# Four steps instead of one for the decays of the first attention group in a hybrid decoder layer

## The chip, the cores and the metric

The kernel runs on one core of a Trainium2 chip. The metric is the device time of one execution in microseconds (us), as the median of several runs. A profile is one execution recorded by the hardware; its span goes from the first to the last instruction of the core. TensorE (PE in the profile) multiplies matrices and writes to PSUM, which has eight tiles here; VectorE (DVE) and ScalarE (ACT) do elementwise work; SyncE (SP) issues most loads. Each engine works through its own queue in order, and they wait for each other through semaphores.

## The reference

One layer of a decoder, for 256 positions of width 2048, in float32: a SwiGLU half-step, a token mixer, a second SwiGLU half-step, each with norms ahead and behind. The mixer projects its input by one wide matrix and runs two causal mixers, GLA (4 heads, key width 128) and HGRN2 (8 heads). The lines that matter here are the decays of GLA:

```
proj = u @ w_in
(g_q, g_k, g_v, g_out, g_code, h_q, h_f, ...) = jnp.split(proj, offsets, axis=-1)
gla_log_a = jax.nn.log_sigmoid(g_code @ gla_w_gk_up + gla_b_gk) / GLA_GATE_NORMALIZER   # 16
o_gla = chunked_gated_linear_attention(split_heads(g_q * (GLA_DK ** -0.5), GLA_HEADS), ...)
```

The kernel works with the decays exp(gla_log_a) themselves, transposed, so that the key dimension lies on the partitions.

## The kernel before, in words

All large products are made in three matmuls of 512 columns: the float32 weights are split into a high part (whi, a copy on ScalarE, L151) and a rest (wlo, a subtraction on VectorE, L153), and so is the activation; `mm3` (L155 to L159) adds high by high (L157), low by high (L158) and high by low (L159).

In the mixer, `gemm_pair` (L329) makes two blocks of 512 output columns in one pass, for both halves of the positions, in four PSUM tiles c00, c10, c01, c11. It runs over the inner dimension in units of 256. A plain step of a unit takes one weight block of 1024 columns (a split on ScalarE, a split on VectorE) and twelve matmuls. Some units, `seven` (L265), use fewer products in the manner of Strassen: 21 matmuls from sums of weight blocks. Such a unit makes `whi` by L278 and L282, the sums `wsum` on VectorE (L243), their high parts `wsumh` on ScalarE (L280 for two thirds, L284 for the last), and then the rests on VectorE, `wlo` twice and `wsuml`. The first `seven` of a pass also takes four more PSUM tiles, p1, p6, p5 and p7 (L291 to L293), and with c they are all eight. So whatever side work holds in these four tiles has to be read out before the first products on p can start. The weights land in a ring of five raw tiles (`raw`, loaded by SP: L133 for a plain block, L272 to L275 for the four blocks of a `seven`), and a raw tile is free for the next load when its split on VectorE is done.

Side work is written as Python generators. `Side.spawn` (L61) runs a generator to its first `yield`; each `side.pump()` (L65), which stands behind the steps of the matmul loops, lets every light generator run on to its next `yield`. So the yields say between which matmul steps a piece of side work is emitted. The framework then orders the instructions of each engine, so the built order of an engine is near to the order of emission but not the same.

Around the change three such generators are light at the same time, during the pass `two(O_GK, O_GV, ...)` (L1167):

- `gla_decays` (L1023): it transposes the 16 code columns (L1035), multiplies them with `gk` (L1043) into two PSUM tiles y, and makes the decays: e = |y| (L1048, ScalarE), m = min(y, 0)/16 (L1050, VectorE), e = exp(-e) (L1053), e = ln(1 + e) (L1055), m = m - e/16 (L1057, VectorE), and fT = exp(m) in four pieces (L1062). A load of ScalarE's function table stands ahead of Ln and another ahead of the second Exp.
- `transposed` (L833), twice, for the queries of the second mixer: four transposes into a PSUM tile (L397) and a copy to hqT on ScalarE (L839).
- `lc_row` (L1082): two matmuls with a matrix of ones (L1093, L1094) into a PSUM tile, and a copy `lcr` (L1096).

Once fT is there, VectorE multiplies the queries of the first mixer with it (qT, L890).

Of the kernel before, what the change touches and what calls it, by code (L numbers as in the profile page):

```python
# [86 lines left out]
def kernel(ctx: ExitStack, tc: tile.TileContext, a: dict, out: bass.AP):  # L87
# [19 lines left out]
    def ps_tile(s="ps"):  # L107
        return psum.tile([P, CB], F32, tag="ps", name=nm(s))
# [292 lines left out]
    def tiles4(x):  # L401
        return x.rearrange("p (k c) -> p k c", c=P)
# [383 lines left out]
    def mixer(x, rs, ready, following):  # L786
        xl = lhs_of(x)
        w_in = a["w_in"]
        with ExitStack() as mctx:
# [5 lines left out]
            def blk(s, dt=F32):  # L795
                return b2.tile([P, CB], dt, tag="b", name=nm(s), bufs=33)
# [33 lines left out]
            def mark(*tiles):  # L830
                laid.update(id(x) for x in tiles)
# [191 lines left out]
            def gla_decays(code, fT):  # L1023


                cs = blk("code")
                for t in range(NT):
                    nc.scalar.activation(cs[:, t * 16:(t + 1) * 16], code[t][:, :16], AF.Copy,
                                         scale=rs[t])
                ct = blk("codeT")  # L1030
                nc.vector.memset(ct[0:17, :NT * P], 1.0)
                yield
                tp = ps_tile()
                for t in range(NT):
                    nc.tensor.transpose(tp[:16, t * P:(t + 1) * P], cs[:, t * 16:(t + 1) * 16], ident)  # L1035
                nc.vector.tensor_copy(ct[0:16, :NT * P], tp[:16, :NT * P])
                yield
                ys = []
                for g in range(2):
                    y = ps_tile()  # L1040
                    for j in range(2):
                        i = 2 * g + j
                        nc.tensor.matmul(y[:, j * 256:(j + 1) * 256], lhsT=gk[:, i * P:(i + 1) * P],  # L1043
                                         rhs=ct[0:17, :NT * P], start=True, stop=True)
                    ys.append(y)
                es, ms = [blk("e") for _ in range(2)], [blk("m") for _ in range(2)]
                for y, e in zip(ys, es):
                    nc.scalar.activation(e, y, AF.Abs)  # L1048
                for y, m in zip(ys, ms):
                    nc.vector.tensor_scalar(m, y, 0.0, 1.0 / GATE_NORMALIZER,  # L1050
                                            op0=ALU.min, op1=ALU.mult)
                for e in es:
                    nc.scalar.activation(e, e, AF.Exp, scale=-1.0)  # L1053
                for e in es:
                    nc.scalar.activation(e, e, AF.Ln, bias=1.0)  # L1055
                for e, m in zip(es, ms):
                    nc.vector.scalar_tensor_tensor(m, e, -1.0 / GATE_NORMALIZER, m,  # L1057
                                                   op0=ALU.mult, op1=ALU.add)
                for g, m in enumerate(ms):
                    mv = m.rearrange("p (h t c) -> p h t c", t=NT, c=P)  # L1060
                    for t in range(NT):
                        nc.scalar.activation(tiles4(fT[t])[:, 2 * g:2 * g + 2, :], mv[:, :, t, :],  # L1062
                                             AF.Exp)
                mark(*fT)
# [51 lines left out]
            side.spawn(operand_sums(x, new_part, sums, False))  # L1116
            hq0 = gemm_block(w_in, O_CODE, 16 + CB, xl)
            side.spawn(gla_decays([hq0[t][0] for t in range(NT)], fT))
            half = (16 + CB) // 2
            for t in range(NT):  # L1120
# [239 lines left out]
```

## Time and profile before

| | |
|---|---|
| runs before, us | 2083.17, 2084.87, 2084.71 |
| median, us | 2084.71 |
| span of the profiled execution, us | 2083.3 |
| instructions | 29324 |
| TensorE busy, us (share of the span) | 2069.5 (99%) |
| VectorE busy, us | 1855.3 (89%) |
| ScalarE busy, us | 1240.8 (60%) |
| mean granted clock of TensorE | 0.998 |
| HBM read and written, MB | 406.11, 4.19 |

The page gives the span of the profiled execution and no other time for it; the median of the runs lies 1.4 us above it. Busy time of TensorE counts matmuls whose ends overlap the next start, so the distance of their starts says more than their durations. In a row of a timeline stand the start in us from the span's start, the duration, the engine, the line, the operation with output and inputs by the names of the program, and in brackets the idle time of the engine ahead of it and what ended it. Waits are listed as who waited for whom, the sum, the count and the longest.

### The profile page before, as it was taken

What the parts mean: (1) busy time and instruction counts of PE and PEld (TensorE: products, weight loads), DVE (VectorE), ACT (ScalarE), POOL (GpSimd) and SP (SyncE); (2) the same over time, 40 slices, a digit from 0 to 9 for tenths busy, and PEclk for the clock granted to TensorE, in tenths of its full rate; (3) what the DMA queues carried; (4) which work ended last, traced back from release to release, by engine and by line L of the source; (5) the groups of instructions that cost most, each with busy time, mean ns of one, the idle gap of its engine ahead of it and who ended that gap; (6) DMA issues with size and microseconds to landing.
All of it is one profiled execution on the core that took longest, in us unless ns stands there. A gap on an engine that the chain in (4) does not pass through costs nothing.

```text
span 2083.3 us, 29324 instructions
## 1 busy us (share of the span) xinstructions
PE 2069.5 (99%) x10509; PEld 1722.0 (83%) x10509; DVE 1855.3 (89%) x2187; ACT 1240.8 (60%) x1670; POOL 40.7 (2%) x87
## 2 busy tenths in 40 slices
PE   9999999999999999999999999999999999999998
PEld 7888888898888888878888888888888888898886
DVE  7898999989899779989999897578999989999896
ACT  6555656566666575576655554465555655666663
POOL 1000000000000100000000000010000000000000
PEclk9999999999999999999999999999999999999999
DMA  8666656667767466555566566755665656576663
GB/s 267 184 209 201 213 187 197 210 185 223 216 191 235 148 201 210 159 172 188 178 195 195 178 220 216 221 182 171 222 197 188 207 187 225 164 238 202 202 206 128
DMA packets 200666, 412.24 MB, mean 198 GB/s; under 512 B 18036, under 2 KB 26423, under 8 KB 200520
## 3 DMA queue, kind: packets, MB, share of 16 engines
q1 hardware_dynamic: 194896, 401.80, 60.9%
q10 hardware_dynamic: 5624, 8.57, 1.4%
q8 instruction: 82, 1.34, 0.3%
q14 instruction: 64, 0.52, 0.1%
HBM read 406.11 MB, written 4.19 MB: 197 GB/s over the span
## 4 chain that ended last, share of the span: by engine, by line
PE 96%; ACT 2%; DVE 1%; issue 1%; DMA 0%; POOL 0%; SPq 0%; DVEq 0%; POOLq 0%; ACTq 0%
PE c L157 22%; PE c L159 21%; PE c L158 21%; PE p L159 5%; PE p L157 5%; PE p L158 5%; PE mm L157 3%; PE mm L159 3%; PE mm L158 3%; PE ps L397 2%; PE acc L157 1%; PE acc L158 1%; PE acc L159 1%; PE ps L905 0%; DVE h L510 0%
## 5 line engine op out<-in xcount | busy, mean ns | idle before, releaser
L151 ACT ACTIVATE whi<-raw 128x1024 fp32r<-128x1024 f32 (+3 forms) x498 | 511.0, 1033 | 284.8 <-PE c L158 116.8
L153 DVE TENSOR_TENSOR wlo<-raw,whi 128x1024 fp32r<-128x1024 f32 (+3 forms) x498 | 587.7, 1190 | 85.5 <-ACT whi L151 84.2
L157 PE MATMUL c<-whi,xhi 128*128 128x512 f32 (+1 forms) x1270 | 495.8, 391 | 0.1
L159 PE MATMUL c<-wlo,xhi 128*128 128x512 f32 (+1 forms) x1270 | 490.9, 387 | 0.0
L158 PE MATMUL c<-whi,xlo 128*128 128x512 f32 (+1 forms) x1270 | 490.6, 386 | 0.0
L243 DVE TENSOR_TENSOR wlo<-raw,whi 128x1024 fp32r<-128x1024 f32 (+1 forms) x252 | 294.5, 1202 | 12.2 <-ACT whi L278 6.1
L159 PEld LDWEIGHTS c<-wlo,xhi 128*128 128x128 f32 x1270 | 238.5, 188 | 47.5 <-DVE wlo L153 0.3
L157 PEld LDWEIGHTS c<-whi,xhi 128*128 128x128 f32 x1270 | 238.6, 188 | 46.3 <-ACT xhi L469 0.5
L158 PEld LDWEIGHTS c<-whi,xlo 128*128 128x128 f32 x1270 | 238.7, 188 | 45.0
L282 ACT ACTIVATE whi<-raw 128x1024 fp32r<-128x1024 f32 (+1 forms) x126 | 131.8, 1046 | 203.9 <-DVE raw L243 80.9
L243 DVE TENSOR_TENSOR wsuml<-wsum,wsumh 128x1536 fp32r<-128x1536 f32 (+1 forms) x126 | 218.1, 1731 | 36.8 <-ACT wsumh L284 36.5
L157 PE MATMUL c<-whi,hkhi 128*128 128x512 f32 x558 | 217.0, 389 | 0.0
L159 PE MATMUL c<-wlo,hkhi 128*128 128x512 f32 x558 | 216.8, 388 | 0.0
L158 PE MATMUL c<-whi,hklo 128*128 128x512 f32 x558 | 216.7, 388 | 0.0
L280 ACT ACTIVATE wsumh<-wsum 128x1024 fp32r<-128x1024 f32 (+1 forms) x126 | 131.6, 1045 | 107.4 <-DVE wsum L243 70.5
L278 ACT ACTIVATE whi<-raw 128x1024 fp32r<-128x1024 f32 (+1 forms) x126 | 131.6, 1044 | 103.0 <-PE c L158 87.7
L243 DVE TENSOR_TENSOR wsum<-raw,raw 128x1024 f32<-128x1024 f32 (+1 forms) x126 | 151.8, 1205 | 21.6 <-DMA raw<-in_ffn_w_down_dram 18.1
L159 PEld LDWEIGHTS c<-wlo,hkhi 128*128 128x128 f32 x558 | 104.7, 188 | 21.6
L158 PEld LDWEIGHTS c<-whi,hklo 128*128 128x128 f32 x558 | 104.7, 188 | 21.4
L157 PEld LDWEIGHTS c<-whi,hkhi 128*128 128x128 f32 x558 | 104.7, 188 | 21.1
L243 DVE TENSOR_TENSOR c<-c,psum 128x512 f32<-128x512 f32 (+1 forms) x135 | 86.5, 683 | 11.8 <-PE c L159 11.4
L243 DVE TENSOR_TENSOR wsum<-raw 128x512 f32<-128x512 f32 (+1 forms) x126 | 86.0, 683 | 3.5
(347 smaller groups left out, 3119.4 us busy)
## 6 DMA issues: line engine op xcount, KB each, us to landing
raw<-in_ffn_w_down_dram SPq DMA_DIRECT2D x124, 512.0 KB, 4.5
raw<-in_w_in_dram SPq DMA_DIRECT2D x104, 512.0 KB, 4.5
raw<-in_ffn_w_up_dram SPq DMA_DIRECT2D x97, 512.0 KB, 4.6
raw<-in_ffn_w_gate_dram SPq DMA_DIRECT2D x96, 512.0 KB, 4.7
raw<-in_ffn_w_gate_dram SPq DMA_DIRECT2D x128, 256.0 KB, 3.7
raw<-in_w_in_dram SPq DMA_DIRECT2D x128, 256.0 KB, 3.5
raw<-in_ffn_w_up_dram SPq DMA_DIRECT2D x126, 256.0 KB, 3.8
raw<-in_ffn_w_down_dram SPq DMA_DIRECT2D x96, 256.0 KB, 4.2
```

What stands on the lines that cost most here:

```text
L151: last[0] = nc.scalar.activation(hi, src, AF.Copy)
L153: nc.vector.tensor_tensor(lo, src, hi.bitcast(F32), op=ALU.subtract)
L157: nc.tensor.matmul(ps, lhsT=xhi, rhs=whi, start=start, stop=False)
L158: nc.tensor.matmul(ps, lhsT=xlo, rhs=whi, start=False, stop=False)
L159: nc.tensor.matmul(ps, lhsT=xhi, rhs=wlo, start=False, stop=stop)
L243: return nc.vector.tensor_tensor(o, x, y, op=op)
L278: nc.scalar.activation(ahi, ra, AF.Copy)
L280: nc.scalar.activation(hi[:, 0:2, :], wsum[:, 0:2, :], AF.Copy)
L282: nc.scalar.activation(bhi, rb, AF.Copy)
L397: end = nc.tensor.transpose(dst_ps[:, i * P:(i + 1) * P], src[:, i * P:(i + 1) * P], ident)
```

## The change

Three yields are put into `gla_decays`. What was emitted as one piece behind the second pump is now emitted in four: the two products, |y| and m; then the first Exp; then Ln; then m and the last Exp. The generators of the queries and of `lc_row`, which come behind it in the list, run their own next pieces in between.

```
@@ -1049,10 +1049,13 @@
                 for y, m in zip(ys, ms):
                     nc.vector.tensor_scalar(m, y, 0.0, 1.0 / GATE_NORMALIZER,
                                             op0=ALU.min, op1=ALU.mult)
+                yield
                 for e in es:
                     nc.scalar.activation(e, e, AF.Exp, scale=-1.0)
+                yield
                 for e in es:
                     nc.scalar.activation(e, e, AF.Ln, bias=1.0)
+                yield
                 for e, m in zip(es, ms):
                     nc.vector.scalar_tensor_tensor(m, e, -1.0 / GATE_NORMALIZER, m,
                                                    op0=ALU.mult, op1=ALU.add)
```

Behind these lines all line numbers are up to 3 higher in the changed kernel (L1057 for Ln, L1060 for m, L1065 for the last Exp, L1099 for lcr). The number behind a name tells tiles of the same name apart, and it can differ between the two builds for the same tile. No instruction is added or taken away on any engine, and SP's order is the same.

ScalarE, in the pass of `two(O_GK, O_GV, ...)`, before, from the first Exp of the decays to the split of the next `seven`; e and fT are the decays, whi_7044 and whi_7046 the high parts of that `seven`:

```order
L1053 ACTIVATE e_6881<-e_6881 128x512
L1055 ACT_TABLE_LOAD
L1055 ACTIVATE e_6880<-e_6880 128x512
L1055 ACTIVATE e_6881<-e_6881 128x512
L278 ACTIVATE whi_7044<-raw_7035 128x1024
L1062 ACT_TABLE_LOAD
L1062 ACTIVATE fT_6439<-m_6882 128x256
L1062 ACTIVATE fT_6440<-m_6882 128x256
L1062 ACTIVATE fT_6439<-m_6883 128x256
L1062 ACTIVATE fT_6440<-m_6883 128x256
L839 COPY hqT_6780<-ps_6898 128x512
L839 COPY hqT_6781<-ps_6904 128x512
```

The same place on ScalarE now:

```order
L1054 ACTIVATE e_6881<-e_6881 128x512
L839 COPY hqT_6780<-ps_6888 128x512
L839 COPY hqT_6781<-ps_6894 128x512
L1099 COPY lcr_6903<-ps_6900 128x512
L1057 ACT_TABLE_LOAD
L1057 ACTIVATE e_6880<-e_6880 128x512
L1057 ACTIVATE e_6881<-e_6881 128x512
L278 ACTIVATE whi_7044<-raw_7035 128x1024
L1065 ACT_TABLE_LOAD
L1065 ACTIVATE fT_6439<-m_6882 128x256
L1065 ACTIVATE fT_6440<-m_6882 128x256
L1065 ACTIVATE fT_6439<-m_6883 128x256
```

The three copies stood behind the last Exp (lcr follows the second copy before as well) and now stand between the first Exp and Ln's table load. Both builds have two table loads here. Behind the Exp group the order is now wsumh_7038 (L280), whi_7046 (L282), wsumh_7038 (L284), whi_7081; before it was whi_7046, whi_7081 and then the two of wsumh_7038.

TensorE, in the same pass, before: the rows from the last product on c ahead of the first products on p6, p5 and p7 (p_1487, p_1488, p_1489) of the pass's first `seven`:

```order
L159 MATMUL c_1452_6832<-wlo_7002,xhi_1326_6187 128x512
L157 MATMUL c_1452_6832<-whi_7001,xhi_1326_6187 128x512
L157 MATMUL p_1487_6975<-whi_6962,xs_6539 128x512
L158 MATMUL p_1487_6975<-whi_6962,xs_6540 128x512
L159 MATMUL p_1487_6975<-wlo_6963,xs_6539 128x512
L157 MATMUL p_1488_6976<-wsumh_6954,xs_6539 128x512
L158 MATMUL p_1488_6976<-wsumh_6954,xs_6540 128x512
L159 MATMUL p_1488_6976<-wsuml_6955,xs_6539 128x512
L157 MATMUL p_1489_6977<-wsumh_6954,xs_6539 128x512
L158 MATMUL p_1489_6977<-wsumh_6954,xs_6540 128x512
L159 MATMUL p_1489_6977<-wsuml_6955,xs_6539 128x512
L158 MATMUL c_1452_6832<-whi_7001,xlo_1327_6188 128x512
```

TensorE now, from the last product on p1 (p_1486) on:

```order
L159 MATMUL p_1486_6968<-wlo_6955,xhi_1311_6092 128x512
L157 MATMUL p_1487_6969<-whi_6956,xs_6539 128x512
L158 MATMUL p_1487_6969<-whi_6956,xs_6540 128x512
L159 MATMUL p_1487_6969<-wlo_6957,xs_6539 128x512
L157 MATMUL p_1488_6970<-wsumh_6948,xs_6539 128x512
L158 MATMUL p_1488_6970<-wsumh_6948,xs_6540 128x512
L159 MATMUL p_1488_6970<-wsuml_6949,xs_6539 128x512
L157 MATMUL p_1489_6971<-wsumh_6948,xs_6539 128x512
L158 MATMUL p_1489_6971<-wsumh_6948,xs_6540 128x512
L159 MATMUL p_1489_6971<-wsuml_6949,xs_6539 128x512
L159 MATMUL c_1452_6832<-wsuml_6949,xhi_1326_6187 128x512
L157 MATMUL c_1450_6830<-whi_7001,xhi_1311_6092 128x512
```

The nine products on p6, p5 and p7 have moved forward by eleven matmuls: they stood among the twelve of the plain step on whi_7001 and now stand right behind the products on p1, ahead of that step. After them come, in both builds, the rest of the twelve on whi_7001, the twelve on whi_7019, and the products of the next `seven`, whose p1 on whi_7044 comes first.

VectorE, before, at the splits of that next `seven`:

```order
L890 TENSOR_TENSOR qT_6437<-qT_6437,fT_6439 128x512
L890 TENSOR_TENSOR qT_6438<-qT_6438,fT_6440 128x512
L243 TENSOR_TENSOR wlo_7047<-raw_7036,whi_7046 128x1024
L153 TENSOR_TENSOR wlo_7082<-raw_7079,whi_7081 128x1024
L243 TENSOR_TENSOR wsuml_7039<-wsum_7037,wsumh_7038 128x1536
L153 TENSOR_TENSOR wlo_7100<-raw_7097,whi_7099 128x1024
L243 TENSOR_TENSOR wsum_7117<-raw_7115,raw_7116 128x1024
```

VectorE now:

```order
L890 TENSOR_TENSOR qT_6437<-qT_6437,fT_6439 128x512
L890 TENSOR_TENSOR qT_6438<-qT_6438,fT_6440 128x512
L243 TENSOR_TENSOR wlo_7047<-raw_7036,whi_7046 128x1024
L243 TENSOR_TENSOR wsuml_7039<-wsum_7037,wsumh_7038 128x1536
L153 TENSOR_TENSOR wlo_7082<-raw_7079,whi_7081 128x1024
L153 TENSOR_TENSOR wlo_7100<-raw_7097,whi_7099 128x1024
L243 TENSOR_TENSOR wsum_7117<-raw_7115,raw_7116 128x1024
```

wsuml_7039 has moved ahead of wlo_7082. Ahead of these rows a third of wsum_7037 is now made ahead of the decays' m instead of behind it. From the end of this pass on, the order of all engines is the same in both builds.

More of the change, by code (lines that the diff above doesn't have):

```diff
@@ L1051, in gla_decays @@
                                             op0=ALU.min, op1=ALU.mult)
+                yield
                 for e in es:
                     nc.scalar.activation(e, e, AF.Exp, scale=-1.0)
+                yield
                 for e in es:
                     nc.scalar.activation(e, e, AF.Ln, bias=1.0)
+                yield
                 for e, m in zip(es, ms):
```

## The prediction

> **What bounds the kernel now.** First the page, busy times by engine, then the waits of TensorE over the whole span (columns: who waited for whom, us in total, times, longest).
>
> ```profile
> PE 2069.5 (99%) x10509; PEld 1722.0 (83%) x10509; DVE 1855.3 (89%) x2187; ACT 1240.8 (60%) x1670; POOL 40.7 (2%) x87
> ```
>
> ```profile
> PE p L157 <- ACT hqT L839: 2.5, 1, 2.5
> PE ps L1300 <- POOL idle L1295: 1.3, 1, 1.3
> PE ps L965 <- ACT state L975: 0.4, 1, 0.4
> ```
>
> TensorE is busy 99% of the span, and it waits three times. The kernel is a queue of matmuls, and an edit moves the end only as far as it moves a start on TensorE. The longest wait, 2.5 us, is for the copies that the change moves. The 1.3 us lie at the program's start, and the 0.4 us belong to another step; neither is touched. Next, the timeline of TensorE around the wait (start, duration, engine, line, operands, idle before).
>
> ```profile
> 759.57 0.40 PE L1094 MATMUL ps<-lcl,ones 128*128 128x512 f32 x1
> ...
> 760.49 0.39 PE L159 MATMUL p<-wlo,xhi 128*128 128x512 f32 x1
> ...
> 763.01 0.39 PE L157 MATMUL c<-whi,xhi 128*128 128x512 f32 x1
> 765.86 0.50 PE L157 MATMUL p<-whi,xs 128*128 128x512 f32 x1 [2.46 <-ACT hqT L839]
> ...
> 766.70 0.63 PE L157 MATMUL p<-wsumh,xs 128*128 128x512 f32 x1
> 767.13 0.63 PE L158 MATMUL p<-wsumh,xs 128*128 128x512 f32 x1
> ...
> 769.69 0.55 PE L159 MATMUL c<-wlo,xhi 128*128 128x512 f32 x1
> 770.07 0.39 PE L157 MATMUL c<-whi,xhi 128*128 128x512 f32 x1
> ```
>
> Matmuls overlap, so what counts is the distance of their starts: from 760.49 to 763.01 there are 11 steps, 0.229 each. From 763.01 to 770.07 there are 12 steps (by the order of TensorE: one product on c, nine on p, two on c), which at 0.229 would take 2.75 us and take 7.06. The disturbance costs 4.31 us. 2.46 of it is the wait. Between 766.70 and 770.07 eight steps take 3.37 us instead of 1.83, so 1.54 are slow matmuls. The remaining 0.31 are the steps beside the wait. The windows say why the eight are slow (columns: stretch and length, busy time and count of PE, PEld, DVE, ACT, POOL, then granted clock, DMA share, GB/s).
>
> ```profile
> 762.00:763.40 1.40, 1.40 (x7) 0.82 (x5) 1.40 (x3) 1.38 (x2) 0.00 (x0) 1.00 0.00 0
> 767.00:768.00 1.00, 1.00 (x4) 0.72 (x4) 0.23 (x1) 1.00 (x2) 0.00 (x0) 0.50 0.19 57
> 769.60:770.00 0.40, 0.40 (x2) 0.31 (x1) 0.40 (x1) 0.40 (x1) 0.00 (x0) 0.50 0.00 0
> 771.00:772.00 1.00, 1.00 (x6) 0.84 (x5) 1.00 (x1) 0.61 (x1) 0.00 (x0) 1.00 1.02 379
> ```
>
> The clock is 1.00 before the wait, 0.50 behind it, and 1.00 again from about 770. Now ScalarE, on which the copies are queued.
>
> ```profile
> 758.13 1.15 ACT L1053 ACTIVATE e<-e 128x512 f32<-128x512 f32 x2
> 759.30 1.28 ACT L1055 ACT_TABLE_LOAD   x1
> 760.59 1.15 ACT L1055 ACTIVATE e<-e 128x512 f32<-128x512 f32 x2
> 761.65 1.05 ACT L278 ACTIVATE whi<-raw 128x1024 fp32r<-128x1024 f32 x1
> 762.71 1.28 ACT L1062 ACT_TABLE_LOAD   x1
> 764.01 1.33 ACT L1062 ACTIVATE fT<-m 128x256 f32<-128x256 f32 x4
> 765.25 1.05 ACT L839 COPY hqT<-ps 128x512 f32<-128x512 f32 x2
> 766.19 0.60 ACT L1096 COPY lcr<-ps 128x512 f32<-128x512 f32 x1
> 766.67 1.07 ACT L282 ACTIVATE whi<-raw 128x1024 fp32r<-128x1024 f32 x1
> 767.62 1.06 ACT L151 ACTIVATE whi<-raw 128x1024 fp32r<-128x1024 f32 x1
> 769.08 1.06 ACT L280 ACTIVATE wsumh<-wsum 128x1024 fp32r<-128x1024 f32 x1 [0.39 <-PE p L158]
> 770.04 0.61 ACT L284 ACTIVATE wsumh<-wsum 128x512 fp32r<-128x512 f32 x1
> ```
>
> There is no idle time from 758.13 to 767.62. The hqT copies empty PSUM tiles that the products p need, and they stand behind two table loads, two Ln, a split and four Exp.
>
> **What goes.** The change puts the three copies ahead of the first table load, and the order holds two loads there before and after, so no function is reloaded. The Exp pair starts at 758.13; a pair's successor starts 1.06 later (760.59 to 761.65), so the first copy starts at 759.19, lcr 0.94 later (765.25 to 766.19) at 760.13, ending at 760.73. Its matmul ends at 759.97 (759.57 + 0.40), so it doesn't wait. On TensorE the nine products on p now follow the step of 760.49: p6 is due at 760.72, p5 at 761.41, p7 at 762.09. The hqT copies end near 759.8 and 760.3 and lcr at 760.73, so each tile is free 0.9 to 1.4 us early. The whole 4.31 us goes: without the wait nothing lowers the clock at this place.
>
> [...]
>
> **What is late next.** The copies take 1.54 us (759.19 to 760.73), and what was ahead of them moves back. The first load starts 0.02 behind the end of its predecessor (758.13 + 1.15 to 759.30), so at 760.75. From there to the end of the Exp group it was 759.30 to 765.25, 5.95, so L280 (wsumh_7038, which now stands first) starts at 766.70 and L282 (whi_7046) 0.96 later (769.08 to 770.04), at 767.66, against 766.67 before. VectorE follows:
>
> ```profile
> 765.07 1.29 DVE L890 TENSOR_TENSOR qT<-qT,fT 128x512 f32<-128x512 f32 x2 [0.78 <-ACT fT L1062]
> 767.77 1.22 DVE L243 TENSOR_TENSOR wlo<-raw,whi 128x1024 fp32r<-128x1024 f32 x1 [1.42 <-ACT whi L282]
> 768.92 1.22 DVE L153 TENSOR_TENSOR wlo<-raw,whi 128x1024 fp32r<-128x1024 f32 x1
> 770.68 1.76 DVE L243 TENSOR_TENSOR wsuml<-wsum,wsumh 128x1536 fp32r<-128x1536 f32 x1 [0.55 <-ACT wsumh L284]
> ```
>
> wlo_7047 started 1.10 after L282 (766.67 to 767.77), so now at 768.76, ending 769.98. The qT pair ahead of it, which waits for fT, starts 1.06 into the Exp group (764.01 to 765.07), now at 766.52, and ends at 767.81: it holds nothing up. wsuml_7039 now comes next, 1.15 later (767.77 to 768.92), at 769.91; its other input, L284, is there by 769.3. It ends at 771.67.
>
> TensorE, in contrast, is 4.31 us earlier. From 760.72, ten products and the 24 on whi_7001 and whi_7019 bring it to 768.51 at the next block's p1. wlo_7047 is wanted eight steps later, at 770.34, its weights one step earlier at 770.11: 0.13 to spare. wsuml_7039 is wanted 14 steps later, at 771.72. A late wsuml is in the trace:
>
> ```profile
> 907.96 1.75 DVE L243 TENSOR_TENSOR wsuml<-wsum,wsumh 128x1536 fp32r<-128x1536 f32 x1
> 909.42 0.39 PE L158 MATMUL p<-wsumh,xs 128*128 128x512 f32 x1
> 909.76 0.50 PE L159 MATMUL p<-wsuml,xs 128*128 128x512 f32 x1
> 910.10 0.40 PE L157 MATMUL p<-wsumh,xs 128*128 128x512 f32 x1
> ```
>
> It ended at 909.71, and the matmul behind the waiting one started 0.39 later. Here that gives 772.06 where 771.95 is due: 0.11 us lost. Since the chain has some ten links, each rounded to hundredths, I take 0.15. All that is queued on TensorE waits with it, but a pause this small didn't bring the slow steps at 909: the next matmul lasts 0.40 there, not 0.63.
>
> Behind that the margins grow, by the windows of the stretch that follows:
>
> ```profile
> 780.00:790.00 10.00, 10.00 (x45) 8.27 (x45) 8.80 (x9) 4.74 (x6) 0.00 (x0) 1.00 0.83 270
> ```
>
> In 10 us at full TensorE, VectorE is busy for 8.80, so it wins back about 1.2 us of cover in each 10. The loads are the other queue that is moved: SP's third load of a block (L274) waits for a split on VectorE.
>
> ```profile
> 764.31 0.33 SPq L274 DMA_DIRECT2D raw<-in_w_in_dram  x1
> raw<-in_w_in_dram SPq DMA_DIRECT2D x14, 256.0 KB, 3.6
> ```
>
> It is issued with the end of wlo_7045, about 1.2 us later than before, at 765.5, and lands 3.6 us on, near 769.1; the sum that reads it stands behind wsuml_7039 (771.67) and two splits of 1.22 on VectorE. Nothing is lost. The counts of instructions, table loads and bytes stay, and the other reordered rows are off TensorE's path. Bounds of the residual wait: 0 below (it is not negative; a gain beyond 4.31 is excluded since TensorE has no other wait here), 1.3 above, if one more operation of the size of a table load lies in the chain.
>
> **The sum.** The profiled span is 2083.3 us and would become 2079.1 (2083.3 - 4.31 + 0.15). The median of the runs shown, 2084.71, is 1.4 above that span; I carry the difference over: 2084.71 - 4.16 = 2080.55, forecast 2080.6, 0.2% less. A difference of 0.2%, 4.2 us, is about what a measurement of this kernel can tell from none, so the forecast falls on that line.
>
> **The rivals.** (1) The wait comes back larger, at wsuml_7039. For it: its cover is below zero in my sum. Against it: each link is a row. With 1.28 more on ScalarE, 0.15 + 1.28 = 1.43 lost: 2081.8. 8%. [...] The order's two loads speak against it.
>
> (2) Slower: the same wait grows until it lowers the clock. Price: lateness L, plus 0.15, plus 1.54. It decides at L = 2.6 us, two table loads of 1.28; every 1 us above is 1 us slower than before, and 0.2% slower needs L = 6.8 (2088.9). For it: VectorE takes qT and wlo in order behind fT. Against: the order shows no added load and ScalarE has no free choice. 3%.
>
> (3) The slow stretch is not the wait's doing, or not every execution has it. Then 1.54 is not won: 2084.71 - 4.31 + 1.54 + 0.15 = 2082.1. For it: the runs shown lie 1.7 us apart (2083.17 and 2084.87), about the size of the slow stretch. [...] 6%.
>
> (4) It doesn't do what it says: p waits for something other than the copies, 2084.7. The trace names hqT, and p began 0.61 behind the first copy's start (765.25 to 765.86), about one copy. 3%.
>
> **Numbers.** The forecast's case has 80%, half of it on either side of the line: its residual can fall to nothing (2080.4), and medians shift by some tenths. Faster 0.40; same 0.40 + 0.08 + 0.06 + 0.03 = 0.57; slower 0.03. Range: below 2080.4 by 0.8, half of the spread of the runs shown, 2079.6; above to the third rival and half a us, 2082.6.
>
> **What would show it.** In the changed profile: the wait of p for hqT gone from TensorE's waits; hqT copies near 759.2; L1057's load near 760.75; granted clock 1.00 from 760 to 775; p1 on whi_7044 near 768.5; at most a wait of some tenths for wsuml near 771.7. A second stretch at 0.50, a third table load, or waits on TensorE of more than 1 us between 768 and 790 would make it wrong.

## The result and the profile after

The changed kernel takes 2080.25 us (median of 13 runs, 2080.01 to 2080.81), the kernel before 2084.43 us beside it (13 runs, 2083.17 to 2085.57). The ratio is 0.9981, with a 95% interval of 0.9973 to 0.9989: 4.18 us or 0.2% less. The interval lies below 1, so the kernel is faster, but by so little that it counts as the same. The forecast was 2080.6 us. The profiled execution of the changed kernel took 2080.67 us, 2078.8 of them span.

First the page of the changed kernel, busy times by engine, then its waits of TensorE over the whole span (who waited for whom, us in total, times, longest).

```profile
PE 2067.8 (99%) x10509; PEld 1721.1 (83%) x10509; DVE 1854.7 (89%) x2187; ACT 1239.7 (60%) x1670; POOL 40.6 (2%) x87
```

```profile
PE ps L1303 <- POOL idle L1298: 1.3, 1, 1.3
PE ps L965 <- ACT state L975: 0.4, 1, 0.4
PE c L157 <- DVE hq L849: 0.3, 1, 0.3
PE ps L1307 <- DMA ident<-in_c_ident_dram: 0.2, 1, 0.2
```

The wait for hqT is gone from the list. The first two are the old ones. The last two are small, lie far from the decays, and come and go between executions of either kernel. Every engine does as much work as before. ScalarE at the place of the change (start, duration, engine, line, operands):

```profile
758.63 1.15 ACT L1054 ACTIVATE e<-e 128x512 f32<-128x512 f32 x2
759.68 1.06 ACT L839 COPY hqT<-ps 128x512 f32<-128x512 f32 x2
760.66 0.59 ACT L1099 COPY lcr<-ps 128x512 f32<-128x512 f32 x1
761.26 1.28 ACT L1057 ACT_TABLE_LOAD   x1
762.56 1.15 ACT L1057 ACTIVATE e<-e 128x512 f32<-128x512 f32 x2
...
764.68 1.28 ACT L1065 ACT_TABLE_LOAD   x1
765.97 1.34 ACT L1065 ACTIVATE fT<-m 128x256 f32<-128x256 f32 x4
767.22 1.04 ACT L280 ACTIVATE wsumh<-wsum 128x1024 fp32r<-128x1024 f32 x1
768.16 1.04 ACT L282 ACTIVATE whi<-raw 128x1024 fp32r<-128x1024 f32 x1
```

The copies stand between the first Exp and Ln's table load, there are still two loads, and what was ahead of the copies has moved back by their length. The times are 0.5 us later than forecast throughout (L1054 at 758.63 against 758.13 before), since this execution was already that much later when it came here; the distances are the forecast ones (L1054 to L1057's load 2.63, forecast 2.62; to L282 9.53, forecast 9.53). VectorE and TensorE behind it:

```profile
767.04 1.29 DVE L890 TENSOR_TENSOR qT<-qT,fT 128x512 f32<-128x512 f32 x2 [1.12 <-ACT fT L1065]
769.24 1.23 DVE L243 TENSOR_TENSOR wlo<-raw,whi 128x1024 fp32r<-128x1024 f32 x1 [0.91 <-ACT whi L282]
770.38 1.75 DVE L243 TENSOR_TENSOR wsuml<-wsum,wsumh 128x1536 fp32r<-128x1536 f32 x1
```

```profile
761.15 0.40 PE L159 MATMUL p<-wlo,xhi 128*128 128x512 f32 x1
761.39 0.39 PE L157 MATMUL p<-whi,xs 128*128 128x512 f32 x1
...
769.10 0.39 PE L157 MATMUL p<-whi,xhi 128*128 128x512 f32 x1
...
772.04 0.39 PE L158 MATMUL p<-wsumh,xs 128*128 128x512 f32 x1
772.27 0.42 PE L159 MATMUL p<-wsuml,xs 128*128 128x512 f32 x1
772.52 0.40 PE L157 MATMUL p<-wsumh,xs 128*128 128x512 f32 x1
```

p6 starts one step behind the last product on p1, where the forecast put it. The next block's p1 follows 7.95 behind that product (forecast 8.02). wsuml ends at 772.13, just too late: from 772.04 to 772.52 two steps take 0.48, where steps of 0.227 (35 of them take the 7.95) would take 0.45. The residual is a few hundredths here; 0.15 was forecast. In a second execution of the same kernel (after_again) the same two steps are later:

```profile
771.85 0.39 PE L158 MATMUL p<-wsumh,xs 128*128 128x512 f32 x1
772.16 0.50 PE L159 MATMUL p<-wsuml,xs 128*128 128x512 f32 x1
772.49 0.39 PE L157 MATMUL p<-wsumh,xs 128*128 128x512 f32 x1
```

They take 0.64 instead of 0.45, so 0.19 are lost. The windows of the stretch in the first execution (granted clock third from the end of a row) show no slow matmul:

```profile
767.00:768.00 1.00, 1.00 (x6) 0.81 (x6) 0.96 (x2) 1.00 (x3) 0.00 (x0) 1.00 0.86 240
768.00:769.00 1.00, 1.00 (x6) 0.84 (x5) 0.33 (x1) 1.00 (x2) 0.00 (x0) 1.00 0.71 266
769.00:770.00 1.00, 1.00 (x6) 0.81 (x5) 0.76 (x1) 1.00 (x3) 0.00 (x0) 1.00 0.00 0
```

Six matmuls start in each us, at a clock of 1.00, where the kernel before had four at 0.50 in its first profile.

### The profile page after: what moved, and what is told of

Same layout as the page of the kernel before. It is cut to its first block, busy times and chain, and to the rows that moved or that the text cites. A ratio compares the mean times of both kernels' runs of the same rounds, so it can differ in the third digit from the quotient of the medians.

```text
span 2078.8 us, 29319 instructions
## 1 busy us (share of the span) xinstructions
PE 2067.8 (99%) x10509; PEld 1721.1 (83%) x10509; DVE 1854.7 (89%) x2187; ACT 1239.7 (60%) x1670; POOL 40.6 (2%) x87
## 4 chain that ended last, share of the span: by engine, by line
PE 96%; ACT 1%; DVE 1%; issue 0%; DMA 0%; POOL 0%; SPq 0%; DVEq 0%; POOLq 0%; ACTq 0%
PE c L157 22%; PE c L159 21%; PE c L158 21%; PE p L159 5%; PE p L158 5%; PE p L157 5%; PE mm L157 3%; PE mm L159 3%; PE mm L158 3%; PE ps L397 2%; PE acc L157 1%; PE acc L158 1%; PE acc L159 1%; PE ps L905 0%; DVE h L510 0%
## 5 line engine op out<-in xcount | busy, mean ns | idle before, releaser
L282 ACT ACTIVATE whi<-raw 128x1024 fp32r<-128x1024 f32 (+1 forms) x126 | 131.8, 1046 | 204.5 <-DVE raw L243 78.5
L280 ACT ACTIVATE wsumh<-wsum 128x1024 fp32r<-128x1024 f32 (+1 forms) x126 | 131.5, 1044 | 108.6 <-DVE wsum L243 74.7
```

The costliest lines, as they stand in the source:

```text
L280: nc.scalar.activation(hi[:, 0:2, :], wsum[:, 0:2, :], AF.Copy)
L282: nc.scalar.activation(bhi, rb, AF.Copy)
```

## The experiments

The theory: 4.31 us of the kernel before are lost at one place, because copies that empty PSUM tiles stand behind table loads on ScalarE; 2.46 are the wait itself, most of the rest is the clock, which falls because TensorE stands still; behind the change there is no slack left for wsuml and wlo. Rivals: the slow stretch has another cause or isn't in every execution; it is the splitting of the decays, not the place of the copies, that counts; the change won slack rather than used it.

All times are medians in us, the ratio is to the kernel before with its 95% interval, and the waits are those of TensorE in the profiled execution.

| kernel | time | runs | ratio | longest wait at the place | granted clock there |
|---|---|---|---|---|---|
| the change | 2080.25 | 13 | 0.9981 (0.9973 to 0.9989) | none | 1.00 |
| late_copies | 2081.56 | 11 | 0.9988 (0.9979 to 0.9996) | hqT 0.8 | 1.00 |
| copies_first | 2084.63 | 11 | 0.9999 (0.9990 to 1.0009) | lcr 2.3 | 0.50 |
| delay_1 | 2081.23 | 11 | 0.9985 (0.9977 to 0.9994) | wlo 0.5 | 1.00 |
| delay_3 | 2083.68 | 11 | 0.9999 (0.9990 to 1.0008) | whi 1.8 | 0.50 (1.00 in a second profile) |
| fill_24 | 2086.64 | 11 | 1.0011 (1.0002 to 1.0020) | none | 1.00 |
| copies_on_dve | 2081.08 | 11 | 0.9985 (0.9976 to 0.9994) | hqT 0.6 | 1.00 |

**The copies one table load later.** Only the third of the change's yields is kept: the decays stop once, behind Ln.

```diff
                 for e in es:
                     nc.scalar.activation(e, e, AF.Ln, bias=1.0)
+                yield
                 for e, m in zip(es, ms):
```

> Only the third yield is kept, so the three copies stand between Ln and the table load of the last Exp. By my theory (what counts is when the three copies have emptied the PSUM tiles of p) the first copy ends at about 762.2 where p6 is due at 761.2 on the clock of the profile before: a wait of about 1.1 us and 0.2 beside it, so about 1.3 us slower than the change, 2081.5. If such a wait also halves the clock, about 1.5 us more, 2083.0. The rival, that splitting the decays is what helps wherever the copies stand, gives 2080.3.

Measured: 2081.56 us. The waits of TensorE and ScalarE's timeline of this kernel:

```profile
PE p L157 <- ACT hqT L839: 0.8, 1, 0.8
```

```profile
759.58 1.28 ACT L1055 ACT_TABLE_LOAD   x1
...
761.93 1.06 ACT L839 COPY hqT<-ps 128x512 f32<-128x512 f32 x2
762.88 0.60 ACT L1097 COPY lcr<-ps 128x512 f32<-128x512 f32 x1
```

Ahead of the second load but still behind the first, the copies come 2.35 behind the start of Ln's load. That is late enough for a wait of 0.8; in its one profile no slow stretch follows. Where the copies stand sets the time: 1.31 us lie between the medians of the two places. By the order of the program, the first yield alone or the second alone gives the order of the change on TensorE, ScalarE, VectorE and SP; these two weren't run.

**The decays undivided, two of the copies ahead.** The decays are spawned behind the transposes instead of ahead of them.

```diff
-            side.spawn(gla_decays([hq0[t][0] for t in range(NT)], fT))
...
             hqT = spawn_T(hqs, "hqT")
+            side.spawn(gla_decays([hq0[t][0] for t in range(NT)], fT))
```

> The decays are one piece as before, but they are spawned behind the two query generators. The two hqT copies then stand even earlier than in the change (ahead of the absolute values), while lcr still stands behind the last Exp. By my theory all three copies count: p7 is due at about 764.4 and lcr ends at 766.8, so TensorE waits about 2.4 us for lcr and may see the half clock behind it; the time is about that before, 2083.5 to 2085. A rival holds that the two hqT copies, which the profile before names, are all: 2080.3. The rival that splitting itself helps gives the time before, 2084.4, with the old wait for hqT.

Measured: 2084.63 us, as before the change. The waits of TensorE, and the windows of this kernel:

```profile
PE p L157 <- ACT lcr L1096: 2.3, 1, 2.3
```

```profile
768.00:769.00 1.00, 1.00 (x5) 0.81 (x4) 0.56 (x2) 1.00 (x2) 0.00 (x0) 0.72 0.43 166
769.00:770.00 1.00, 1.00 (x4) 0.71 (x4) 0.76 (x2) 1.00 (x3) 0.00 (x0) 0.50 0.00 0
770.00:771.00 1.00, 1.00 (x4) 0.81 (x3) 1.00 (x1) 1.00 (x2) 0.00 (x0) 0.50 0.23 29
771.00:772.00 1.00, 1.00 (x5) 0.77 (x4) 1.00 (x2) 0.81 (x1) 0.00 (x0) 0.57 0.70 184
```

The hqT copies come out early, so p6 and p5 run from 760.99 on, but the lcr copy, whose PSUM tile p7 needs, still stands behind the last Exp, and the wait moves on to it nearly whole. All three copies have to be out; two don't help. The clock falls again behind the wait, which here ends at p7 (767.55).

**Is there slack behind the change?** Here, and in the next one, in-place copies of e (128x512, the values unchanged) stand ahead of Ln in the changed kernel and delay all that follows on ScalarE: two copies in the first, 1.06 us by estimate, as the two of Ln take in the profile before (760.59 to 761.65).

```diff
                 yield
+                for _ in range(1):
+                    for e in es:
+                        nc.scalar.activation(e, e, AF.Copy)
                 for e in es:
                     nc.scalar.activation(e, e, AF.Ln, bias=1.0)
```

> The change with two more copies of 128x512 in place (e to e) on ScalarE between the three copies and Ln: about 1.06 us more in the chain. By my sum wsuml of the next block is at the edge of its cover, so the whole 1.06 us comes back as a wait for wlo and wsuml: 2081.3. The rival, that there is slack, gives 2080.3.

Measured: 2081.23 us, 0.98 above the change. The waits of TensorE:

```profile
PE c L159 <- DVE wlo L243: 0.5, 1, 0.5
```

Of the estimated 1.06 us of delay 0.98 arrive at the end, 0.52 of it as this wait and the rest in the steps beside it and at wsuml. From p1's last product to the last matmul it is 1309.87 (760.38 to 2070.25), 0.9 and 1.1 above the two profiles of the change (below). So the chain through the decays to the next block's splits has hardly any slack behind the change, as the sum had it (0.13 for wlo, below zero for wsuml). What it is delayed by shows as a pause of TensorE: 0.52 us here, 1.79 and 0.30 with the six copies below.

**More delay.** The same with six copies (`range(3)`), some 3.2 us by the same estimate (three times 1.06), once timed and once more for its profile alone.

> The change with six more such copies, about 3.2 us more in the chain. By my theory TensorE waits about 3 us at wlo and wsuml of the next block: 2083.4 without, 2084.9 with a stretch of half clock behind the wait. With slack in the chain it would be less. If the slow stretch of before has nothing to do with a wait, it is absent here: 2083.4 in every run.

> The delayed chain once more. Its runs fall near 2083.4 and near 2085.2. By my theory an execution near 2083.4 shows the same wait of about 2 us without the stretch at 0.50, and one near 2085.2 shows it.

Measured: 2083.68 us, but in two groups: 7 runs from 2083.26 to 2083.91 and 4 from 2084.85 to 2085.41. The first profiled execution took 2085.31, the second 2083.68. Both have the same wait, here a row of TensorE's timeline of the second:

```profile
772.20 0.50 PE L157 MATMUL c<-whi,xhi 128*128 128x512 f32 x1 [1.79 <-ACT whi L282]
```

In the first execution the clock is 0.50 from 774 to 777, in the second it is 1.00 throughout. From the last product on p1 to the last matmul the first takes 1313.00 us (760.87 to 2073.87) and the second 1311.34 (760.96 to 2072.30). So the slow stretch costs about 1.7 us, and the same wait has it in one execution and not in another.

Two things came out otherwise than expected. TensorE was to wait some 3 us at wlo and wsuml; it waits 1.79 at whi and 0.30 at wlo, and its order isn't that of the change here: a product on p6 stands ahead of the last of the three on c at the wait. And without the stretch only 2.4 to 2.6 of the estimated 3.2 us of delay arrive at the last matmul (1311.34 against 1308.97 and 1308.73). That the lower runs still lie where they were expected, 3.1 above the change, owes some 0.7 to the stores at the end (below), so it is partly luck.

**The wait filled with matmuls.** In the kernel before, 24 matmuls by a matrix of zeros are added on a c tile ahead of the first p6; the value of c is unchanged. ScalarE does what it did, but TensorE doesn't stand still.

```diff
             side.pump()
+            if zeros and "p6" not in self.begun:
+                z = zeros.pop()
+                for _ in range(24):
+                    nc.tensor.matmul(self.c[0][0][:, :self.w], lhsT=z, rhs=second[1][0],
+                                     start=False, stop=False)
             self.product("p6", self.part("s2", u), second[0], end)
```

> Before, with 24 matmuls by a zero matrix added onto c in the pass (they change no value), most of them right ahead of the products on p. They fill the time in which TensorE waited for hqT: p6 is due at about 765.76, the copy is out at 765.82. By my theory (the idle time brings the half clock) there is no stretch at 0.50 and no second group of slower runs; behind p6 the order has 13 matmuls more than before (13 x 0.229 = 3.0), so 3.0 above the faster group of before (2083.3), less 0.2 beside the wait: 2086.1 in all runs. The rival, that the slow stretch belongs to this place and not to the wait, gives two groups, 2086.1 and 2087.6, and the stretch at 0.50 in the profile.

> The filled kernel once more. With no wait for hqT there is no stretch at 0.50 near the products on p, whatever the time of the run; the rival that the stretch belongs to the place shows it in some executions.

Measured: 2086.64 us (2085.86 to 2087.37, one group), and 2087.30 in the second execution that was profiled. TensorE's timeline in the first:

```profile
760.56 5.21 PE L302 MATMUL c<-whi,zero 128*128 128x512 f32 x22
765.73 0.50 PE L158 MATMUL p<-whi,xs 128*128 128x512 f32 x1
...
2074.89 0.39 PE L160 MATMUL c<-held,hkhi 128*128 128x512 f32 x1
```

p6 is as late as before the change, but there is no idle time ahead of it, and neither profile has a slow stretch. That alone would be little, since two of the four profiles of the kernel before have none either (below), and the runs, one group 1.5 us wide, don't tell. From p1's last product to the end of the matmuls it is 1314.55 (760.34 to 2074.89) and 1314.32 (761.69 to 2076.01). Two of the 24 stand ahead of that product and two matmuls on c behind it in their stead, so 24 are taken off, at 0.227: 1309.1 and 1308.9, what the change takes (below). All fourteen profiles together say more. Seven have a wait of TensorE of 1.8 to 2.5 us around here, for hqT, lcr or whi, and in four of them (before, before_again_2, copies_first, delay_3) the stretch at 0.50 begins 0.6 to 1.8 us behind the wait's end, wherever the wait stands. The other seven, with no wait here above 0.84, have none. So the slow stretch hangs on TensorE's standing still; with fourteen profiles that is well supported, not certain. The median is 0.5 above the 2086.1 expected, and 0.94 above the change's 2080.25 and 24 matmuls (5.45); most of that lies behind the last matmul (below).

**The copies on VectorE.** The decays stay in one step, and the three copies are made by VectorE, in whose queue no table load stands.

```diff
-                nc.scalar.copy(dst, tp)
+                if on_dve:
+                    nc.vector.tensor_copy(dst, tp)
+                else:
+                    nc.scalar.copy(dst, tp)
...
-                nc.scalar.copy(lc_rows[g], ps)
+                (nc.scalar.copy if g else nc.vector.tensor_copy)(lc_rows[g], ps)
...
-            hqT = spawn_T(hqs, "hqT")
+            hqT = spawn_T(hqs, "hqT", True)
```

> The decays in one piece as before, the three copies (hqT twice, lcr) made by VectorE instead of ScalarE. VectorE makes them behind m, from about 763.1 on, 0.6 each; p6 is due at 763.0. By my theory the wait is 0.8 us and 0.2 beside it: 2081.1 to 2081.4. The rival, that the split of the decays is what helps, gives the time before, 2084.4.

Measured: 2081.08 us, 0.8 above the change. The waits of TensorE:

```profile
PE p L157 <- DVE hqT L840: 0.6, 1, 0.6
```

Most of the gain comes without splitting anything, and with p6 still behind ten other matmuls after p1 in TensorE's order (eleven in the kernel before), so the place behind the table loads was the fault. VectorE is the fuller engine (89% against 60%) and gives the copies back 0.6 late, so the change's way is the better one here.

**Does every execution of the kernel before have the slow stretch?** Three more executions of it and one of the changed kernel were profiled.

> The kernel before once more, for a second profile. The runs of before fall into two groups, near 2083.3 and near 2084.7. If the half clock behind the wait makes the difference, an execution of the faster group shows the same wait of 2.5 us without the stretch at 0.50, and one of the slower group shows it; by the rival that the groups come from elsewhere both show it.

> As before_again_1: a third profile of the kernel before, with the wait of 2.5 us, and with or without the stretch at 0.50 by its group.

> A fourth profile of the kernel before. From the first product on p6 to the last matmul it should take about 1306.2 us if the granted clock stays at 1.00 behind the wait, as in before_again_1, and about 1307.7 with the stretch at 0.50. By the rival that the groups of runs come from elsewhere, that distance does not go with the clock.

> The changed kernel once more: no wait for hqT, the granted clock at 1.00 from 750 to 790, at most some tenths of a us at wsuml; about 2080.3.

Measured: 2084.38, 2085.33 and 2083.17 us, and 2080.74 for the changed kernel. TensorE in the second of the three, then its windows:

```profile
760.88 0.39 PE L159 MATMUL p<-wlo,xhi 128*128 128x512 f32 x1
...
766.12 0.50 PE L157 MATMUL p<-whi,xs 128*128 128x512 f32 x1 [2.35 <-ACT hqT L839]
...
767.06 0.63 PE L157 MATMUL p<-wsumh,xs 128*128 128x512 f32 x1
...
2073.93 0.39 PE L159 MATMUL c<-held,hkhi 128*128 128x512 f32 x1
```

```profile
766.00:767.00 1.00, 0.88 (x3) 0.75 (x4) 0.62 (x2) 1.00 (x4) 0.00 (x0) 0.88 0.96 344
767.00:768.00 1.00, 1.00 (x4) 0.75 (x3) 0.00 (x0) 1.00 (x3) 0.00 (x0) 0.50 0.40 141
768.00:769.00 1.00, 1.00 (x4) 0.81 (x3) 0.97 (x1) 0.94 (x1) 0.00 (x0) 0.50 0.00 0
769.00:770.00 1.00, 1.00 (x3) 0.76 (x3) 1.00 (x2) 0.57 (x1) 0.00 (x0) 0.50 0.00 0
770.00:771.00 1.00, 1.00 (x5) 0.81 (x4) 0.39 (x1) 1.00 (x3) 0.00 (x0) 0.92 0.66 66
```

And TensorE in the third:

```profile
760.45 0.40 PE L159 MATMUL p<-wlo,xhi 128*128 128x512 f32 x1
...
765.68 0.50 PE L157 MATMUL p<-whi,xs 128*128 128x512 f32 x1 [2.34 <-ACT hqT L839]
...
766.48 0.39 PE L157 MATMUL p<-wsumh,xs 128*128 128x512 f32 x1
...
2071.79 0.39 PE L159 MATMUL c<-held,hkhi 128*128 128x512 f32 x1
```

The wait is the same, 2.35 and 2.34 us, but in the third the matmuls behind it last 0.39 instead of 0.63 and the clock is 1.00 throughout. The first of the three (wait of 2.32) has no slow stretch either. The third rival holds in its second half: not every execution has the stretch. Its first half, that the stretch isn't the wait's doing, is left without support by the filled wait and by the stretch that moves with the wait.

A partial miss: 33 runs of the kernel before fall in two heaps (10 from 2083.01 to 2083.44, 23 from 2083.97 to 2085.70), and I expected them to tell which execution had the stretch. The 34 runs of two other sets have six in the gap (2083.56 to 2083.93), so the heaps aren't clean. The first of the three profiles has no stretch and yet took 2084.38. It waited 0.8 us for hklo and 0.5 us for the identity matrix elsewhere, which the third didn't. Only the profile tells the two apart.

## Why the prediction was right, and where by luck

The distance from p1's last product to the last matmul leaves out what happens ahead of the place and behind TensorE's end:

| execution | from | to | distance |
|---|---|---|---|
| before, as profiled first (stretch at 0.50) | 760.49 | 2073.52 | 1313.03 |
| before_again_2 (stretch at 0.50) | 760.88 | 2073.93 | 1313.05 |
| before_again_1 (none) | 761.73 | 2073.11 | 1311.38 |
| before_again_3 (none) | 760.45 | 2071.79 | 1311.34 |
| the change | 761.15 | 2069.88 | 1308.73 |
| after_again | 760.97 | 2069.94 | 1308.97 |

- **What goes.** Against the execution that the prediction was made from, the change wins 4.30 us between these points in one profile and 4.06 in the other; the sum had 4.16, which is 4.31 less 0.15. Right in its mechanism and its size.
- **The split into wait and slow clock.** The stretch costs 1313.04 - 1311.36 = 1.68 us (two executions each), 1.54 were put down to it. The windows of before_again_2 show why: with 0.24 us of the first and 0.16 of the last of the five at half rate, the slow time is 3.40 us, of which half is lost. The prediction counted only eight of its steps as slow and had the rest in the 0.31 beside the wait. Where an execution has no stretch, the change wins 2.4 to 2.6 (1311.36 less 1308.97 or 1308.73).
- **The copies' place and cover.** L1057's load at 2.63 behind Exp (2.62), two table loads, p6 right behind p1 without a wait: all as forecast.
- **The residual.** The place was right, wsuml's weights, and the forecast 0.15 lies between the 0.03 and 0.19 of the two profiles. What was taken from the rows at 909 held in the first: the matmul behind the waiting one starts 0.39 behind wsuml's end (772.13 to 772.52). delay_1 shows the edge: 0.98 of the estimated 1.06 us come through. Rival 1, a wait of another table load, would have needed about what delay_1 added by hand.
- **Rival 2,** a wait that grows until it lowers the clock, isn't what the change does. delay_3 shows the mechanism: a wait of 1.79, less than the 2.46 of before, and the stretch in one of its two profiles. The forecast had the gain eaten up at a lateness of 2.6, with the stretch. The execution of delay_3 that has the stretch is there: it is 2.5 late without it (1313.00 less 1308.85, the mean of the change's two, less 1.68) and takes 1313.00, as the kernel before takes 1313.03. The median of its runs is the time before as well (ratio 0.9999, 0.9990 to 1.0008).
- **From the span to the median.** This step agreed partly by luck. The prediction took 4.16 from the median as if every execution had the stretch and the ends were equal. Two terms were missing. The stretch isn't in every execution, which makes the gain at the place smaller in those. And behind the last matmul the profiles differ: from its start to the end of the span, the four executions of before take 9.49 to 9.78 us, the two of the changed kernel 8.92 and 8.96. What differs is the landing of the last two stores on SP's queue, in the rows of the DMA issues behind 2070 us (count, size of one, median us to landing), first of before_again_3, then of the changed kernel:

```profile
out_dram<-h SPq DMA_DIRECT2D x2, 256.0 KB, 2.8
```

```profile
out_dram<-h SPq DMA_DIRECT2D x2, 256.0 KB, 2.1
```

The change doesn't touch these stores. copies_first, with the order of ScalarE's decays as before, has 2.1 there, delay_3 has 2.8 in both its executions. So it stays with a kernel, but not with the change's idea, and why is open. It is worth 0.7 us (means of 9.64 and 8.94). It is in fill_24 too: behind its last matmul come 9.51 and 9.49, some 0.6 more than in the changed kernel. Ahead of the place the four executions of before lie up to 1.3 us apart (760.45 to 761.73), the two of the changed kernel 0.2. The wait and the stores together give some 3.2 us (2.5 and 0.7), with the stretch 4.9; the median's 4.18 lies between, as a mixture of executions with and without it would. In what share of the runs the stretch was, nothing here shows.

How long the stretch is can be worked out from the granted clock of the windows, with the share at 0.50 of the first and the last one: 3.42 us in the first profile of before (766.60 to 770.02) and in copies_first (768.44 to 771.86), 3.40 in before_again_2 (766.76 to 770.16) and in delay_3 (773.90 to 777.30). Waits of 1.79 to 2.46 us were followed by it in these four executions and not in three others (before_again_1 with 2.32, before_again_3 with 2.34, delay_3_again with 1.79). Waits of 0.84, 0.52 and 0.6 (late_copies, delay_1, copies_on_dve) had no stretch behind them, with one profile each. From which length on the clock falls wasn't tried, and why the same wait has the stretch behind it in one execution and not in another isn't shown.

No version that was run beats the change.

## What to carry to other kernels

When a full TensorE waits, look for what its PSUM tiles or operands are queued behind, on which engine, and move that one link ahead of the long work there; move every copy that the next products need, since lcr left behind alone kept 2.3 of the 2.5 us here (copies_first). Price a wait by its length, and for waits like those of 1.8 to 2.5 us here add up to 1.7 us of slow clock that came in four of seven profiles, so look at several profiles before a gain is counted whole. Measure between two matmuls around the change: what lies ahead of them and behind them differed here by up to 1.3 us between executions and 0.7 between kernels.

## What the runs showed that was not expected

- Behind a TensorE wait of 1.8 to 2.5 us came 3.4 us at a granted clock of 0.50, worth 1.7 us, in four profiles; in three others the clock stayed at 1.00, two of them of the kernel before, with 2.32 and 2.34 against the 2.46 and 2.35 that had it. Matmuls by zeros in place of the idle time kept it at 1.00 in both profiles.
- The runs lie closer together behind the change: 0.8 us for the changed kernel (2080.01 to 2080.81), 2.4 for the one before (2083.17 to 2085.57). A stretch of 1.7 us that comes and goes would make that difference; that it alone does isn't shown.
- The last stores of two kernels with the same final instructions land 2.1 or 2.7 to 2.9 us behind their issue, and several profiles of one kernel agree.
